# Convolution taps moved to ScalarE, and 14 pairs of up panels run with a seven-product block

## The chip, the cores and the metric

One core of one Trainium2 chip runs the whole program. The metric is the device time of one execution in microseconds (us), as the median of several runs. Engines: PE is TensorE, DVE is VectorE, ACT is ScalarE, POOL is GpSimd, SP is SyncE; a q behind a name (ACTq) marks the instruction queue of that engine issuing a transfer.

## The reference

Two decoder layers on 256 tokens of width 2048 in float32: a gated linear attention layer, then a forgetting attention layer, both with attention into 256 memory tokens. After each mixer comes the channel mixer, where the change lies:

```python
def causal_dwconv(u, w, b):
    s_ = u.shape[1]
    up = jnp.pad(u, ((0, 0), (CONV_WIDTH - 1, 0), (0, 0)))
    return w[0] * up[:, 0:s_] + w[1] * up[:, 1:s_ + 1] + w[2] * up[:, 2:s_ + 2] + b

def conv_ffn(h, w_up, conv_w, conv_b, w_down):
    u = causal_dwconv(h @ w_up, conv_w, conv_b)
    a, val = split_cols(u, [FFN_HIDDEN, FFN_HIDDEN])
    return (jax.nn.silu(a) * val) @ w_down
...
        h = rmsnorm(x, norm_ffn[i])
        x = x + conv_ffn(h, ffn_w_up[i], ffn_conv_w[i], ffn_conv_b[i], ffn_w_down[i])
```

The hidden width is 5632, so `w_up` has 11264 columns. Each channel of `u` gets three taps (weights w0, w1, w2 for the tokens two back, one back and the same) and a bias.

## The kernel before

**Units.** All weights stream from HBM as units: two blocks of 128 input features by 512 columns, one transfer of 512 KB into a tile `raw` (4 buffers). ACT rounds a unit to `whi` (L208, a cast to fp32r), DVE takes the rest, `wlo = raw - whi` (L217); `whi` and `wlo` have 3 buffers each. The tokens are held the same way, as a high and a low part. A block product of one 128x128 token block with a 128x512 weight block is then three matmuls (high by high, low by high, high by low), each 128x512. A plain unit has two feature blocks and two token blocks, so 4 block products, 12 matmuls.

**Panels.** A panel is 512 columns of a weight: 8 units for the 2048 input features, accumulated in two PSUM banks `acc` (one per token block; 4 banks in all, so two panels can be open). An up panel holds two blocks of 128 channels of the gate half and the two blocks of the value half that belong to them. There are 22 up panels in each layer; `PARTS` groups them 8, 8 and 6, and each part's down panels follow it.

**What happens to an up panel.** `panel(j, ...)` gives its evacuation: ACT scales both banks by the norm into `scaled` (2 buffers), DVE transposes 32x32 squares into `square`, ACT's queue writes that to DRAM (`turned`), and ACT's queue reads it back as channels by tokens into `u0` or `u1` (four transfers). Then `taken(j, base, u, i)`, once per half, does the convolution: per block one ACT instruction (tap 2 and bias, L1092) and two on DVE (taps 1 and 0, L1093 and L1094), Silu on ACT, the product on DVE, and the split into high and low parts as input of the down panels.

**What sets the order.** Each engine runs its queue strictly in order, and the transfers that ACT issues stand in the same queue as its arithmetic. The order of each queue is made by a list scheduler when the program is built; weight casts have a higher priority. `later((n, step), ...)` lets a step begin only behind the cast of the n-th unit from then: 3 for the write, 6 for the reads, 8 and 9 for the two halves of `taken`.

**Seven for eight.** `proj_seven` runs two panels at once, unit by unit, and uses all 4 `acc` banks. At chosen unit pairs (`forms`) it replaces the 8 block products of the pair by 7 on sums of blocks: 21 matmuls, not 24. Each panel's unit of the pair is loaded, four DVE instructions form the sums `t13` and `t24` (L346 to L349), and 3.5 tiles instead of 2 are cast and split (L314, L315: v0 whole, `vhi`/`vlo` half a tile, `t13`, `t24`). Four of the products go to PSUM banks of their own. `seven_evacuated` copies one of these to SBUF (`s16`), adds the others on DVE, and hands the sums to the evacuation, which adds them to the scaled panel (`extra`). Before the change this is used in the second layer's mixer and, with another ending (`add_seven`), in the down panels. All up panels run alone by `proj_tm` (two of each layer by `proj_two`).

Of the kernel before, what the change touches and what calls it, by code (L numbers as in the profile page):

```python
# [12 lines left out]
F32 = mybir.dt.float32  # L13
F32R = mybir.dt.float32r
I32 = mybir.dt.int32
AF = mybir.ActivationFunctionType
ALU = mybir.AluOpType
# [21 lines left out]
AHEAD = 300  # L39
SEVEN = ((3, 5), (3, 5, 7))  # L40
LAST = ()

SPREAD = [128 * q + 32 * k + i for k in range(4) for i in range(32) for q in range(4)]

# [93 lines left out]
def _trunk(ctx: ExitStack, tc: tile.TileContext, xt, xtok, memt, wp, wgu, gns, gfin, cnv, par, msk, out):  # L138
# [39 lines left out]
    def later(*steps):  # L178

        for units, step in steps:  # L180
            due.append([units, step])
# [267 lines left out]
    def back():  # L449
        return tp.tile([P, 4, T], F32, name="back", tag="back", bufs=2)  # L450
# [612 lines left out]
    def ffn(l, nx, h, m, then, ending=None):  # L1063
        with tc.tile_pool(name=f"ffn{l}", bufs=1) as fp, ExitStack() as ends:
# [11 lines left out]
            held = []  # L1076

            def spare_tile(name, dtype):
                return sp.tile([P, 512 if name in ("vhi", "vlo") else NUNIT], dtype, name=name, tag=name)

            def form(t):
                return lambda i: [t[:, h, i, :] for h in range(2)]

            def taken(j, base, u, i):

                cv = []
                for c in range(2):
                    v = u[:, 2 * c + i, :]
                    col = (c * 44 + j + i) * 4
                    w = [cw[:, col + n : col + n + 1] for n in range(4)]  # L1090
                    r = fp.tile([P, T], F32, name=f"cv{c}", tag=f"cv{c}", bufs=3)
                    S.activation(r, v[:, 2:], AF.Identity, bias=w[3], scale=w[2])  # L1092
                    V.scalar_tensor_tensor(r, v[:, 1 : T + 1], w[1], r, ALU.mult, ALU.add)  # L1093
                    V.scalar_tensor_tensor(r, v[:, :T], w[0], r, ALU.mult, ALU.add)  # L1094
                    cv.append(r)
                S.activation(cv[0], cv[0], AF.Silu)
                V.tensor_tensor(cv[1], cv[0], cv[1], ALU.mult)
                split(m, j + i - base, cv[1])
                if (j - base) // 2 in parts[base]:
                    held.append(cv[1])  # L1100
                    if i:
                        summed(parts[base][(j - base) // 2])

            def summed(form):
                ab = [natural(h)[:, :, b] for h in held for b in range(2)]
                held.clear()
                token_sums(*ab, sp.tile([P, 4, P], F32, name="sf", tag="sf"), [form[:, h, :, :] for h in range(2)])

            def panel(j, base, slack=0):
                held = []  # L1110

                def evac(b, a):
                    if not held:
                        held.append(Turn("turned"))
                    e = tp.tile([P, 512], F32, name="scaled", tag="scaled", bufs=2)
                    S.activation(e, a, AF.Copy, scale=nx.col()[:, b : b + 1])
                    held[0].put(b, e)
                    if not b:
                        return
                    u = us[turn[0] % 2]  # L1120
                    turn[0] += 1
                    later((3, held[0].write), (6, lambda: held[0].read(lambda k: u[:, k, 2:])),
                          (8 + slack, lambda: taken(j, base, u, 0)), (9 + slack, lambda: taken(j, base, u, 1)))

                return evac

            parts = {lo: dict(zip(SEVEN[1] if p < len(PARTS) - 1 else LAST, tiles)) for p, (lo, _) in enumerate(PARTS)}
            for p, (lo, hi) in enumerate(PARTS):
                forms = parts[lo]
                js = list(range(lo, hi, 2))  # L1130
                if not p:
                    proj_two([("up", l, j) for j in js[:2]], h, [panel(js[0], lo), panel(js[1], lo, 2)], 2)
                    js = js[2:]
                for j in js:
                    proj_tm(("up", l, j), h, panel(j, lo))
# [175 lines left out]
```

## Time and profile before

| | |
|---|---|
| time of the runs | median 2241.81 us (2240.89, 2241.81, 2243.47) |
| span of the profiled execution, first to last instruction | 2241.1 us; its time as a run is not listed apart |
| PE busy | 2227.2 us, 99% of the span |
| DVE busy | 1658.5 us, 74% |
| ACT busy | 1294.0 us, 58% |
| DMA | 516.98 MB, mean 231 GB/s |
| granted TensorE clock | 0.999 |

Busy time leaves out instructions that only wait or issue a transfer. Matmuls overlap in the pipeline, so the durations of single matmuls add up to more than the busy time.

### The profile page before, as it was taken

The numbers are of one execution on the slowest core, as the hardware profiler recorded it, in microseconds if no ns is written. First come the engines' busy times: TensorE is split into PE (matmuls) and PEld (weight loads), VectorE is DVE, ScalarE is ACT, GpSimd is POOL, SyncE is SP. The second block draws the span as 40 slices with busy tenths as digits, with TensorE's granted clock in tenths as the row PEclk, the third lists the DMA queues.
The fourth block names the chain that finished last, engine by engine and source line by source line (L and its number), as shares of the span: only waits on it lengthen the run. The fifth ranks groups of instructions, "written<-read, shape, count | busy, mean of one in ns | idle before, by whom it ended". The sixth has DMA issues, their size and how long they took to land.

```text
span 2241.1 us, 29637 instructions
## 1 busy us (share of the span) xinstructions
PE 2227.2 (99%) x10267; PEld 1860.8 (83%) x10267; DVE 1658.5 (74%) x2608; ACT 1294.0 (58%) x1921; POOL 44.6 (2%) x71
## 2 busy tenths in 40 slices
PE   9999999999999999999999999999999999999998
PEld 7888888888888888888888898888888888888886
DVE  7568887667689677886777875666778967787766
ACT  7555665656565465555656655555665555554654
POOL 0000000000000000000000000000000000000000
PEclk9999999999999999999999999999999999999999
DMA  9875667677875778667778777677876677767784
GB/s 319 277 234 188 205 208 224 202 234 242 256 222 201 243 233 249 213 203 246 235 254 263 243 239 222 196 233 244 255 243 220 204 239 244 240 193 233 237 242 150
DMA packets 276894, 516.98 MB, mean 231 GB/s; under 512 B 149884, under 2 KB 158600, under 8 KB 276616
## 3 DMA queue, kind: packets, MB, share of 16 engines
q1 hardware_dynamic: 124296, 427.24, 58.9%
q10 hardware_dynamic: 149760, 80.51, 12.6%
q0 software_dynamic: 2688, 7.34, 1.1%
q8 instruction: 80, 1.31, 0.2%
q14 instruction: 70, 0.57, 0.1%
HBM read 470.44 MB, written 44.58 MB: 230 GB/s over the span
## 4 chain that ended last, share of the span: by engine, by line
PE 95%; DMA 3%; DVE 1%; issue 1%; ACT 0%; SPq 0%; DVEq 0%; ACTq 0%
PE acc L229 24%; PE acc L230 24%; PE acc L233 24%; PE acc L291 16%; PE ps_s L291 1%; DMA back<-xturned 1%; PE ps_o L291 1%; PE ps_t L291 1%; DMA back<-turned 1%; DMA raw<-wp 1%; PE ps_s L833 0%; DMA turned<-square 0%; PE ps_s L634 0%; PE ps_t L623 0%; PE ps_o L645 0%
## 5 line engine op out<-in xcount | busy, mean ns | idle before, releaser
L217 DVE TENSOR_TENSOR wlo<-raw,whi 128x1024 fp32r<-128x1024 f32 (+4 forms) x763 | 912.6, 1199 | 458.0 <-ACT whi L208 429.5
L208 ACT ACTIVATE whi<-raw 128x1024 fp32r<-128x1024 f32 (+4 forms) x763 | 791.2, 1040 | 704.7 <-PE acc L230 471.9
L229 PE MATMUL acc<-whi,B 128*128 128x512 f32 (+3 forms) x1440 | 548.1, 382 | 0.0
L230 PE MATMUL acc<-whi,B 128*128 128x512 f32 (+3 forms) x1440 | 547.9, 382 | 0.0
L229 PE MATMUL acc<-whi,A 128*128 128x512 f32 x1120 | 437.3, 392 | 1.7 <-ACT whi L208 1.4
L230 PE MATMUL acc<-whi,A 128*128 128x512 f32 x1120 | 435.4, 390 | 0.0
L233 PE MATMUL acc<-wlo,B 128*128 128x512 f32 (+3 forms) x1440 | 377.0, 381 | 0.0
L229 PEld LDWEIGHTS acc<-whi,B 128*128 128x128 f32 x1440 | 270.3, 188 | 46.9
L230 PEld LDWEIGHTS acc<-whi,B 128*128 128x128 f32 x1440 | 269.9, 188 | 46.3
L233 PEld LDWEIGHTS acc<-wlo,B 128*128 128x128 f32 x1440 | 267.7, 188 | 46.4
L233 PE MATMUL acc<-wlo,A 128*128 128x512 f32 x1120 | 300.6, 390 | 0.3 <-DVE wlo L217 0.3
L229 PEld LDWEIGHTS acc<-whi,A 128*128 128x128 f32 x1120 | 210.3, 188 | 48.1 <-ACT whi L208 3.6
L233 PEld LDWEIGHTS acc<-wlo,A 128*128 128x128 f32 x1120 | 210.1, 188 | 44.3 <-DVE wlo L217 0.7
L230 PEld LDWEIGHTS acc<-whi,A 128*128 128x128 f32 x1120 | 210.3, 188 | 43.5 <-DVE A L527 0.2
L291 PE MATMUL acc<-whi,B 128*128 128x512 f32 x508 | 132.2, 390 | 0.0
L291 PE MATMUL acc<-whi,A 128*128 128x512 f32 x496 | 129.9, 390 | 0.0
L291 PEld LDWEIGHTS acc<-whi,B 128*128 128x128 f32 x508 | 95.1, 188 | 20.3
L1092 ACT ACTIVATE cv<-u,cw 128x256 f32<-128x256 f32 x176 | 96.8, 588 | 23.9 <-DMA u<-turned 23.9
L291 PEld LDWEIGHTS acc<-whi,A 128*128 128x128 f32 x496 | 93.1, 188 | 19.9
L314 ACT ACTIVATE whi<-t 128x1024 fp32r<-128x1024 f32 x46 | 48.9, 1062 | 79.2 <-DVE t L349 42.7
L1093 DVE SCALAR_TENSOR_TENSOR cv<-u,cw,cv 128x256 f32<-128x256 f32 x176 | 78.5, 479 | 15.6 <-ACT cv L1092 15.6
L438 DVE STREAM_TRANSPOSE square<-scaled 128x512 f32<-128x512 f32 x122 | 80.3, 692 | 0.0
(259 smaller groups left out, 1819.5 us busy)
## 6 DMA issues: line engine op xcount, KB each, us to landing
raw<-wp SPq DMA_DIRECT2D x743, 512.0 KB, 4.2
turned<-square ACTq DMA_DIRECT2D x61, 512.0 KB, 4.5
u<-turned ACTq DMA_DIRECT2D x176, 128.0 KB, 5.2
raw<-wp SPq DMA_DIRECT2D x32, 384.0 KB, 3.2
raw<-wp SPq DMA_DIRECT2D x24, 388.0 KB, 3.9
xturned<-square ACTq DMA_DIRECT2D x12, 512.0 KB, 4.3
back<-xturned ACTq DMA_DIRECT2D x40, 128.0 KB, 5.6
raw<-wp SPq DMA_DIRECT2D x8, 400.0 KB, 3.8
```

The lines of the kernel that those rows point to most:

```text
L208: casts.append(S.activation(hi[:, s], raw[:, s], AF.Copy))
L217: V.tensor_tensor(lo[:, s], raw[:, s], hi[:, s].bitcast(F32), ALU.subtract)
L229: TE.matmul(acc[:, :n], xh, hi[:, s], start=first and j == 0, stop=False)
L230: TE.matmul(acc[:, :n], xl, hi[:, s], start=False, stop=False)
L233: TE.matmul(a, xh, ls, start=False, stop=stop)
L291: TE.matmul(a[:, :n], x, w, start=k not in begun, stop=calls[k] == 0)
L314: casts.append(S.activation(hi, raw, AF.Copy))
L438: V.transpose(self.square[:, :, :, b], src.rearrange("p (c t) -> p c t", t=32))
L1092: S.activation(r, v[:, 2:], AF.Identity, bias=w[3], scale=w[2])
L1093: V.scalar_tensor_tensor(r, v[:, 1 : T + 1], w[1], r, ALU.mult, ALU.add)
```

## The change

Two things change in `ffn`, which both layers use.

The taps: a panel is now handled in whole tiles of 4 blocks. `begun` makes tap 2 with the bias into a tile `a` and tap 1 into a tile `b`, eight ACT instructions of 128x256, and one DVE addition of 128x1024; `taken` makes tap 0 into `b` (four more on ACT), adds it (DVE), and does Silu and product on half tiles of 128x512. `a` and `b` are the two buffers of `back`. The instructions with two constants are L1105, those with one L1107, the additions L1114 and L1119, Silu L1120, product L1121.

The pairs: after the first two up panels of a layer, up panels run two by two through `seven_evacuated`, the fifth unit pair (u = 4) with seven products, until two panels of the part are left, which run alone. That is 2, 3 and 2 pairs in the three parts of a layer, 14 in all. `mixed` holds the sums of token blocks that the seven products need, made once per layer. The two panels of a pair are written, read and tapped with two units more distance for the second (`slack`).

```diff
--- before.py
+++ after.py
@@ -39,6 +39,7 @@
 AHEAD = 300
 SEVEN = ((3, 5), (3, 5, 7))
 LAST = ()
+UP = (4,)
 
 SPREAD = [128 * q + 32 * k + i for k in range(4) for i in range(32) for q in range(4)]
 
@@ -1076,30 +1077,54 @@
             held = []
 
             def spare_tile(name, dtype):
-                return sp.tile([P, 512 if name in ("vhi", "vlo") else NUNIT], dtype, name=name, tag=name)
+                return sp.tile([P, NUNIT if name in ("t13", "t24") else 512], dtype, name=name, tag=name)
 
             def form(t):
-                return lambda i: [t[:, h, i, :] for h in range(2)]
-
-            def taken(j, base, u, i):
-
-                cv = []
+                return lambda i: [t[:, k, i, :] for k in range(2)]
+
+            mixed = [sp.tile([P, 2, 4, P], F32R, name=f"mixed{i}") for i in range(len(UP))]
+
+            def mixed_at(u, t):
+                def step():
+                    f, g = (tp.tile([P, 512], F32, name=n, tag="scaled", bufs=2) for n in ("sf", "sh"))
+                    sums_of(h, (2 * u, 2 * u + 1), f.rearrange("p (i t) -> p i t", t=P),
+                            g.rearrange("p (c t) -> p c t", t=T), [t[:, k, :, :] for k in range(2)])
+
+                return step
+
+            later(*[(18 + 2 * i, mixed_at(u, t)) for i, (u, t) in enumerate(zip(UP, mixed))])
+
+            def taps(t, u, j, n):
+
                 for c in range(2):
-                    v = u[:, 2 * c + i, :]
-                    col = (c * 44 + j + i) * 4
-                    w = [cw[:, col + n : col + n + 1] for n in range(4)]
-                    r = fp.tile([P, T], F32, name=f"cv{c}", tag=f"cv{c}", bufs=3)
-                    S.activation(r, v[:, 2:], AF.Identity, bias=w[3], scale=w[2])
-                    V.scalar_tensor_tensor(r, v[:, 1 : T + 1], w[1], r, ALU.mult, ALU.add)
-                    V.scalar_tensor_tensor(r, v[:, :T], w[0], r, ALU.mult, ALU.add)
-                    cv.append(r)
-                S.activation(cv[0], cv[0], AF.Silu)
-                V.tensor_tensor(cv[1], cv[0], cv[1], ALU.mult)
-                split(m, j + i - base, cv[1])
-                if (j - base) // 2 in parts[base]:
-                    held.append(cv[1])
-                    if i:
-                        summed(parts[base][(j - base) // 2])
+                    for i in range(2):
+                        k = 2 * c + i
+                        col = (c * 44 + j + i) * 4
+                        g = [cw[:, col + m : col + m + 1] for m in range(4)]
+                        if n == 2:
+                            S.activation(t[:, k, :], u[:, k, 2:], AF.Identity, bias=g[3], scale=g[2])
+                        else:
+                            S.activation(t[:, k, :], u[:, k, n : T + n], AF.Copy, scale=g[n])
+
+            def begun(j, u, got):
+                a, b = back(), back()
+                got += [a, b]
+                taps(a, u, j, 2)
+                taps(b, u, j, 1)
+                V.tensor_tensor(a, a, b, ALU.add)
+
+            def taken(j, base, u, got):
+                a, b = got
+                taps(b, u, j, 0)
+                V.tensor_tensor(a, a, b, ALU.add)
+                S.activation(a[:, :2, :], a[:, :2, :], AF.Silu)
+                V.tensor_tensor(a[:, 2:, :], a[:, :2, :], a[:, 2:, :], ALU.mult)
+                for i in range(2):
+                    split(m, j + i - base, a[:, 2 + i, :])
+                u = (j - base) // 2
+                if u in parts[base]:
+                    held.extend(a[:, 2 + i, :] for i in range(2))
+                    summed(parts[base][u])
 
             def summed(form):
                 ab = [natural(h)[:, :, b] for h in held for b in range(2)]
@@ -1109,18 +1134,20 @@
             def panel(j, base, slack=0):
                 held = []
 
-                def evac(b, a):
+                def evac(b, a, extra=None):
                     if not held:
                         held.append(Turn("turned"))
                     e = tp.tile([P, 512], F32, name="scaled", tag="scaled", bufs=2)
                     S.activation(e, a, AF.Copy, scale=nx.col()[:, b : b + 1])
+                    if extra is not None:
+                        V.scalar_tensor_tensor(e, extra, nx.col()[:, b : b + 1], e, ALU.mult, ALU.add)
                     held[0].put(b, e)
                     if not b:
                         return
-                    u = us[turn[0] % 2]
+                    u, got = us[turn[0] % 2], []
                     turn[0] += 1
                     later((3, held[0].write), (6, lambda: held[0].read(lambda k: u[:, k, 2:])),
-                          (8 + slack, lambda: taken(j, base, u, 0)), (9 + slack, lambda: taken(j, base, u, 1)))
+                          (8 + slack, lambda: begun(j, u, got)), (9 + slack, lambda: taken(j, base, u, got)))
 
                 return evac
 
@@ -1130,6 +1157,10 @@
                 js = list(range(lo, hi, 2))
                 if not p:
                     proj_two([("up", l, j) for j in js[:2]], h, [panel(js[0], lo), panel(js[1], lo, 2)], 2)
+                    js = js[2:]
+                while len(js) > 2:
+                    seven_evacuated([("up", l, j) for j in js[:2]], h, {u: form(t) for u, t in zip(UP, mixed)},
+                                    [panel(js[0], lo), panel(js[1], lo, 2)], spare_tile)
                     js = js[2:]
                 for j in js:
                     proj_tm(("up", l, j), h, panel(j, lo))
```

The instruction counts of the program: PE 9988 matmuls before, 9946 now; ACT 1788 and 2140; DVE 501 and 205 SCALAR_TENSOR_TENSOR, 1625 and 1823 TENSOR_TENSOR; transfers unchanged (SP 864, ACT 368).

How the queues change is shown at two places of the first layer's part 1: the handling of its first up panels, which before lies beside the next panels' plain units, and now beside the second pair of that part. Numbers behind names count buffers; `u0` and `u1` hold the panels, `cw` the taps' weights, `turned` is the DRAM copy.

First the queue of ACT. Before, from the write of a panel to the Silu of its first half:

```order
L441 DMA turned_6940<-square_6939 128x1024
L208 ACTIVATE whi_7023<-raw_7022 128x1024
L208 ACTIVATE whi_7041<-raw_7040 128x1024
L446 DMA u0_4583<-turned_6940 128x4x64 x4
L208 ACTIVATE whi_7063<-raw_7062 128x1024
L208 ACTIVATE whi_7081<-raw_7080 128x1024
L1092 ACTIVATE cv0_7086<-u0_4583,cw_4581 128x256
L1092 ACTIVATE cv1_7090<-u0_4583,cw_4581 128x256
L208 ACTIVATE whi_7121<-raw_7120 128x1024
L1092 ACTIVATE cv0_7126<-u0_4583,cw_4581 128x256
L1092 ACTIVATE cv1_7130<-u0_4583,cw_4581 128x256
L1096 ACTIVATE cv0_7086<-cv0_7086 128x256
```

Now, from the write of the first panel of the first pair to the last read of the second:

```order
L442 DMA turned_7140<-square_7139 128x1024
L209 ACTIVATE whi_7256<-raw_7255 128x1024
L447 DMA u0_4583<-turned_7140 128x4x64 x2
L442 DMA turned_7168<-square_7167 128x1024
L447 DMA u0_4583<-turned_7140 128x4x64 x2
L209 ACTIVATE whi_7278<-raw_7277 128x1024
L209 ACTIVATE whi_7300<-raw_7299 128x1024
L1105 ACTIVATE back_7305<-u0_4583,cw_4581 128x256 x2
L1107 ACTIVATE back_7306<-u0_4583,cw_4581 128x256 x2
L447 DMA u1_4584<-turned_7168 128x4x64 x3
L209 ACTIVATE whi_7329<-raw_7328 128x1024
L447 DMA u1_4584<-turned_7168 128x4x64
```

and on, through the fifth unit pair of the second pair:

```order
L1105 ACTIVATE back_7305<-u0_4583,cw_4581 128x256
L1107 ACTIVATE back_7306<-u0_4583,cw_4581 128x256
L1105 ACTIVATE back_7305<-u0_4583,cw_4581 128x256
L1107 ACTIVATE back_7306<-u0_4583,cw_4581 128x256
L315 ACTIVATE whi_7371<-raw_7361 128x1024
L315 ACTIVATE vhi_7375<-raw_7363 128x512
L1107 ACTIVATE back_7306<-u0_4583,cw_4581 128x256 x4
L315 ACTIVATE whi_7388<-t13_7365 128x1024
L1120 ACTIVATE back_7305<-back_7305 128x512
L381 ACTIVATE s16_7419<-ps_t_7357 128x512
L315 ACTIVATE whi_7398<-t24_7366 128x1024
```

Between the write and the first read stood two casts and stands one. Behind the reads stood the four taps of a panel with one cast between them; now twelve taps, the reads and the write of the other panel, Silu and `s16` stand among the casts of the fifth to the tenth unit (`whi_7256` to the cast of `t24`).

Then the queue of DVE at the same place. Before:

```order
L217 TENSOR_TENSOR wlo_7084<-raw_7080,whi_7081 128x1024
L1093 SCALAR_TENSOR_TENSOR cv0_7086<-u0_4583,cw_4581,cv0_7086 128x256
L1093 SCALAR_TENSOR_TENSOR cv1_7090<-u0_4583,cw_4581,cv1_7090 128x256
L1094 SCALAR_TENSOR_TENSOR cv0_7086<-u0_4583,cw_4581,cv0_7086 128x256
L1094 SCALAR_TENSOR_TENSOR cv1_7090<-u0_4583,cw_4581,cv1_7090 128x256
L217 TENSOR_TENSOR wlo_7124<-raw_7120,whi_7121 128x1024
L1093 SCALAR_TENSOR_TENSOR cv0_7126<-u0_4583,cw_4581,cv0_7126 128x256
L1093 SCALAR_TENSOR_TENSOR cv1_7130<-u0_4583,cw_4581,cv1_7130 128x256
L1097 TENSOR_TENSOR cv1_7090<-cv0_7086,cv1_7090 128x256
L1094 SCALAR_TENSOR_TENSOR cv0_7126<-u0_4583,cw_4581,cv0_7126 128x256
L1094 SCALAR_TENSOR_TENSOR cv1_7130<-u0_4583,cw_4581,cv1_7130 128x256
```

Now:

```order
L1114 TENSOR_TENSOR back_7305<-back_7305,back_7306 128x1024
L347 TENSOR_TENSOR t13_7365<-raw_7363,raw_7361 128x512
L348 TENSOR_TENSOR t13_7365<-raw_7363 128x512
L316 TENSOR_TENSOR wlo_7372<-raw_7361,whi_7371 128x1024
L316 TENSOR_TENSOR vlo_7376<-raw_7363,vhi_7375 128x512
L349 TENSOR_TENSOR t24_7366<-raw_7363,t13_7365 128x512
L1119 TENSOR_TENSOR back_7305<-back_7305,back_7306 128x1024
L316 TENSOR_TENSOR wlo_7389<-t13_7365,whi_7388 128x1024
L350 TENSOR_TENSOR t24_7366<-raw_7361,t24_7366 128x512
L1121 TENSOR_TENSOR back_7305<-back_7305 128x512
L316 TENSOR_TENSOR wlo_7399<-t24_7366,whi_7398 128x1024
```

The eight short tap instructions are gone; two additions of whole tiles stand ahead of `t13` and between the two steps of `t24`, on which the last cast of the fifth unit pair waits.

## The prediction

> **What bounds the kernel now.** I read the first part of the page, then the chain of work that ended last, then a window over the first layer's up and down panels.
>
> ```profile
> span 2241.1 us, 29637 instructions
> PE 2227.2 (99%) x10267; PEld 1860.8 (83%) x10267; DVE 1658.5 (74%) x2608; ACT 1294.0 (58%) x1921; POOL 44.6 (2%) x71
> ...
> PE 95%; DMA 3%; DVE 1%; issue 1%; ACT 0%; SPq 0%; DVEq 0%; ACTq 0%
> ```
>
> PE is never out of work and is 95% of the chain. The window from 512 to 1130 us (columns: window, length, then busy time and count of PE, weight loads, DVE, ACT, POOL; clock, DMA share, GB/s) gives the price of a matmul, and four plain up panels what DVE and ACT do beside it:
>
> ```profile
> 512.00:1130.00 618.00, 618.00 (x2722) 510.64 (x2721) 471.20 (x657) 357.44 (x471) 0.00 (x0) 1.00 0.74 232
> ...
> sum 85.33, PE 85.33 PEld 70.64 DVE 63.66 ACT 52.66 POOL 0.00; mean PE 21.33 PEld 17.66 DVE 15.92 ACT 13.17 POOL 0.00
> ```
>
> 618.00 us over 2722 matmuls is 0.227 us each, without a gap and at full clock. So a plain unit of 12 matmuls takes 2.72 us, and in this stretch only fewer matmuls can make the kernel faster, while every wait of PE makes it slower. The second row sums four panels (560.87 to 646.2 us): per panel DVE is busy 15.9 and ACT 13.2 of 21.3 us.
>
> **What the change removes.** 14 pairs times 3 matmuls are 42, as the program's count also says (9988 to 9946): 42 x 0.227 = **9.5 us** less on the path that sets the end. The profiled execution's span is 2241.1 us, 0.7 under the median of the runs; with every cost hidden the median would become 2232.3.
>
> **What it adds beside PE.** Prices come from places where instructions follow each other without idle time, start to start, since neighbours overlap by about 0.1 us. First ACT's timeline in a plain panel and in the second layer:
>
> ```profile
> 595.81 1.08 ACT L1092 ACTIVATE cv<-u,cw 128x256 f32<-128x256 f32 x2
> 596.80 0.40 ACT L1096 ACTIVATE cv<-cv 128x256 f32<-128x256 f32 x1
> 597.11 1.04 ACT L208 ACTIVATE whi<-raw 128x1024 fp32r<-128x1024 f32 x1
> ...
> 603.52 0.34 ACTq L441 DMA_DIRECT2D turned<-square  x1
> 604.51 1.06 ACT L208 ACTIVATE whi<-raw 128x1024 fp32r<-128x1024 f32 x1 [1.66 <-PE acc L230]
> 607.23 1.06 ACT L208 ACTIVATE whi<-raw 128x1024 fp32r<-128x1024 f32 x1 [1.66 <-PE acc L230]
> 608.41 2.14 ACTq L446 DMA_DIRECT2D u<-turned  x4
> ...
> 1234.20 1.05 ACT L208 ACTIVATE whi<-raw 128x1024 fp32r<-128x1024 f32 x1
> 1235.15 0.93 ACT L526 ACTIVATE A<-back,gains 128x256 fp32r<-128x256 f32 x2
> 1235.98 1.05 ACT L208 ACTIVATE whi<-raw 128x1024 fp32r<-128x1024 f32 x1
> ```
>
> A tap with two constants is 0.495 us (two in 0.99), one with one constant 0.415 (two of the like L526 in 0.83), a cast of a unit 0.95, a read 0.53 (four in 2.14). Half a cast I take as 0.53, the 0.63 of `vhi` below less the overlap. The read at 608.41 came 4.9 us behind its write at 603.52. Then DVE's, at a seven-product pair and at the end of a pair in the second layer:
>
> ```profile
> 1263.01 0.75 DVE L481 SCALAR_TENSOR_TENSOR scaled<-ps_t,ny,scaled 128x512 f32<-128x512 f32 x1
> 1263.67 0.74 DVE L481 SCALAR_TENSOR_TENSOR scaled<-s,ny,scaled 128x512 f32<-128x512 f32 x1
> 1264.34 0.71 DVE L438 STREAM_TRANSPOSE square<-scaled 128x512 f32<-128x512 f32 x1
> ...
> 1294.08 0.68 DVE L348 TENSOR_TENSOR t<-raw,t 128x512 f32<-128x512 f32 x1
> 1294.68 1.22 DVE L315 TENSOR_TENSOR wlo<-raw,whi 128x1024 fp32r<-128x1024 f32 x1
> 1295.82 0.68 DVE L349 TENSOR_TENSOR t<-raw,t 128x512 f32<-128x512 f32 x1
> 1296.42 2.52 DVE L315 TENSOR_TENSOR wlo<-t,whi 128x1024 fp32r<-128x1024 f32 x2
> ...
> L1093 DVE SCALAR_TENSOR_TENSOR cv<-u,cw,cv 128x256 f32<-128x256 f32 x176 | 78.5, 479 | 15.6 <-ACT cv L1092 15.6
> ```
>
> A whole tile of tensor by tensor is 1.14 us, half a tile 0.60, a scaled addition 0.67, an old tap 0.45 (78.5 us over 176).
>
> Per panel ACT gets 8 one-constant taps: +3.3 us; DVE loses 8 old taps (3.6) and gains two whole-tile additions (2.3): -1.3. Per pair the seven products cost ACT 1.5 casts and `s16` (0.95 + 0.53 + 0.5 = 2.0) and DVE four sums, 1.5 splits, four additions and four scaled additions (2.4 + 1.7 + 2.4 + 2.7 = 9.2). Reads and writes already cost ACT's queue about 2.5 us a panel. So in a pair's 189 x 0.227 = 42.9 us ACT has 2 x (13.2 + 2.5 + 3.3) + 2.0 = 40.0 us of work, before 31.4, and DVE 2 x (15.9 - 1.3) + 9.2 = 38.4, before 31.8. Both still fit; the average does not stop PE. The cover is thin, though, and both queues are strictly in order, so the place where things meet decides. SP's and POOL's queues keep their instructions. The sums `mixed`, 2 or 3 us of DVE once per layer, lie in the first plain panels and cost nothing beside 15.9 of 21.3.
>
> **The place: the fifth unit pair.** How the end of a pair passes shows where the second layer already has one (L479 is ACT's scaling of a finished panel, L441 the write, L446 a read), with PE's first matmul of the next pair:
>
> ```profile
> 1265.14 0.69 ACT L479 ACTIVATE scaled<-acc,ny 128x512 f32<-128x512 f32 x1 [0.63 <-DVE square L438]
> ...
> 1266.81 0.34 ACTq L441 DMA_DIRECT2D turned<-square  x1
> ...
> 1272.42 1.04 ACTq L446 DMA_DIRECT2D fkt<-turned  x2
> 1273.50 1.31 ACTq L441 DMA_DIRECT2D turned<-square  x1
> 1274.86 0.63 ACT L314 ACTIVATE vhi<-raw 128x512 fp32r<-128x512 f32 x1 [4.86 <-DVE t L346]
> ...
> 1264.16 1.07 PE L291 MATMUL acc<-whi,A 128*128 128x512 f32 x4
> ```
>
> Count from the next pair's first matmul, 1264.16. The write stands at +2.7, the reads at +8.3: ACT stood 4.86 us behind a read that waited for the write to land. It cost PE nothing there, since no taps followed. How long these transfers take over the kernel (last number, us to landing), and the writes in the window from 512 to 1130 us; and the idle time of PE (last number) ahead of the matmuls of pairs:
>
> ```profile
> turned<-square ACTq DMA_DIRECT2D x61, 512.0 KB, 4.5
> u<-turned ACTq DMA_DIRECT2D x176, 128.0 KB, 5.2
> ...
> DMA to landing us min/median/max: 2.4/4.9/9.9
> ...
> L291 PE MATMUL acc<-whi,B 128*128 128x512 f32 x508 | 132.2, 390 | 0.0
> ```
>
> Now I walk the new order of part 1's second pair with these prices, in us from that pair's first matmul. Before the write stand the evacuation of the second panel and a cast that needs the first unit's buffer (free at +2.3): write at +3.4. Landed, by 4.9, at +8.3. First two reads, second panel's write, two more reads: to +10.7. Casts of units 6 and 7: to +12.6. First tap at 8.3 + 5.2 = +13.5; four taps 1.8: +15.3. Three reads of the second panel, the first under the last tap: +16.6. Cast of unit 8: +17.55. Four taps: **+19.4**. Only now can DVE begin its row: addition 1.14, the two steps of `t13` 1.2, split 1.14, half split 0.6, first step of `t24` 0.6, second addition 1.14, split of `t13` 1.14, second step of `t24` 0.6, in all 7.56: +27.0. The cast of `t24`, 0.95 and a tenth to be seen: **+28.0**. PE wants it behind 8 units and 14 matmuls, 110 x 0.227 = +24.95. PE so waits **3.1 us**, and the time is not regained, for in the rest of the pair PE has no slack. DVE's own 7.56 us leave nothing to hide: had the taps ended by +16.3, PE would not wait.
>
> The same sequence (addition, `t13`, `t24` around the second addition) stands in DVE's queue at four pairs of each layer, those that follow another pair: 8 x 3.1 = **24.8 us**. Their two kinds differ a little: at the third pair of part 1 the write stands behind one cast more, about 0.5 us later, with no cast between it and the reads. The first pair of a layer follows `proj_two`, whose first panel is finished 5.4 us earlier; its addition stands well ahead, and a late Silu between the steps of `t24` may cost 0 to 1.5, I take 0.8: 1.6 for both. The first pairs of the other two parts, four in all, meet no taps: 0.
>
> **The plain panels behind a pair.** The taps of a pair's second panel fall into the first plain panel, 6 such places. There casts have their usual cushion (3 buffers, about 5 us) and no sum to wait for, but ACT carries 13.2 + 2.5 + 3.3 = 19.0 of 21.8 us and two panels' reads. The trace shows no such load. From below the cost is 0, as in every plain panel now; from above it is one landing less the cushion that is left, 2 us. I take 1: **6 us**. Where the taps meet down panels, the walk leaves casts just in time: 0, up to 1 each.
>
> **The sum.** -9.5 + 24.8 + 1.6 + 6 = +22.9; 2241.8 + 22.9 = **2265 us**, 1.0% slower.
>
> **Rivals.** (1) *The gain arrives*, 2232.3 us. It takes one thing: the round trip through DRAM (4.9 + 5.2 us in my walk) shorter by 3.1 us, so that the taps end by +16.3. For it: a landing as short as 2.4 us occurs, and PE has not waited at a pair until now (0.0 in the L291 row). Against: the medians 4.5 and 5.2, the 4.9 at 603.52 and 5.6 at 1266.81. From the point where the wait is 1.2 us a pair, 9.5 us in all with nothing else, the gain wins. The Trainium skill, "DMA: Bandwidth & Descriptors", section "Anatomy of one DMA", gives a transfer as 2.0 us plus its bytes by 436 GB/s (a fit for the GpSimd path): by that page an estimate of 3.2 us for the write and 2.3 for a read, 4.6 less than my round trip, and the kernel would be faster. The rows above disagree with it for these small-piece transfers in a busy stretch, so I give this rival little. (2) *Even*: a wait of about 1.2 us a pair, 2242. Halfway values of the landing do that. (3) *Worse*: ACT at 19.0 of 21.8 us also fails in the plain panels and down panels (14 places more at 2 to 3 us): 2265 + 35 = 2300. For it: each late read stops casts behind it. Against: 5 us of cushion. That the change takes out fewer matmuls than said is excluded by the count.
>
> **How the numbers follow.** The forecast, waits of 2 to 5 us at the eight pairs, 0.58: from -9.5 + 16 + 0 + 2 = +8.5 to -9.5 + 40 + 3 + 10 = +43, so 2250 to 2285. The gain 0.15, even 0.12, worse 0.15. Faster by over 0.2% (about what this kernel's measurement can tell from no change, 4.5 us) 0.15, within it 0.12, slower 0.73. The range reaches down to the whole gain, 2233, and up to 2292 in the worse case.
>
> **What the next profile would show.** If right: PE's pitch still 0.227, its count 42 lower; idle time of PE ahead of matmuls with `whi` or `ps_o` at the cast line of `t24` (now L315), released by ACT, about 3 us each at eight places; ACT's queue standing behind `u<-turned` some 5 us behind each write; DVE in one run of 7 to 8 us from the first whole-tile addition to the second step of `t24`. If the reads follow their writes by 3 us or less, or the first addition ends before +17 of a pair, I am wrong at the landing; if DVE idles between the addition and `t24`, at the order.

## The result and the profile after

The changed kernel takes **2274.7 us** (median; 2271.1 to 2279.8), the kernel before 2242.6 (2240.9 to 2244.3) in the same comparison: a ratio of **1.014**, 95% interval 1.0126 to 1.0155. It is slower, by 32 us of the medians and 28.2 of the profiled spans, where 23 were forecast. The page of the profiled execution, its first part and the chain of work that ended last:

```profile
span 2269.3 us, 29661 instructions
...
PE 2232.2 (98%) x10225; PEld 1853.6 (82%) x10225; DVE 1749.1 (77%) x2510; ACT 1446.1 (64%) x2273; POOL 44.6 (2%) x71
...
PE 82%; DMA 5%; DVE 5%; ACT 5%; issue 2%; ACTq 1%; SPq 0%; DVEq 0%
```

The 42 matmuls are gone (10267 before; both traces count 279 more than the program's own list of matmuls). PE's share of the chain fell from 95% to 82%: stretches of the chain now run through DVE, ACT and transfers, though PE is still busy 98% of the span. That is the look of many short waits.

To size them I add up, from the trace, the start-to-start distances of successive matmuls beyond a full-speed pitch of 0.2268 us. This excess is 24.8 us before and 62.3 after: +37.5, less 42 x 0.227 = 9.5, is +28.0, which is the spans' 28.2. I split it into the **eight** fifth unit pairs of the pairs that follow a pair (from 4 us ahead of the first product with `mixed` to 3 us behind the last) and the **rest**. After, the eight hold 24.9 us and the rest 37.4, 12.6 more than before.

One of the eight, part 1's second pair, whose first matmul is at 773.03 us. A selection of its timeline (start, duration, engine, line; in brackets the idle time ahead and what ended it), with rows of ACT, DVE and PE in order of time:

```profile
775.63 0.34 ACTq L442 DMA_DIRECT2D turned<-square  x1
781.49 0.93 ACTq L447 DMA_DIRECT2D u<-turned  x2
785.31 2.01 ACT L209 ACTIVATE whi<-raw 128x1024 fp32r<-128x1024 f32 x2 [6.43 <-DMA raw<-wp]
787.48 1.13 ACT L1105 ACTIVATE back<-u,cw 128x256 f32<-128x256 f32 x2 [0.16 <-DMA u<-turned]
...
793.39 0.49 ACT L1107 ACTIVATE back<-u,cw 128x256 f32<-128x256 f32 x1
793.91 1.23 DVE L1114 TENSOR_TENSOR back<-back 128x1024 f32<-128x1024 f32 x1 [0.56 <-ACT back L1107]
795.06 0.69 DVE L347 TENSOR_TENSOR t<-raw 128x512 f32<-128x512 f32 x1
796.26 1.22 DVE L316 TENSOR_TENSOR wlo<-raw,whi 128x1024 fp32r<-128x1024 f32 x1
797.53 0.50 PE L292 MATMUL ps_t<-wlo,B 128*128 128x512 f32 x1 [0.98 <-DVE wlo L316]
798.60 1.22 DVE L1119 TENSOR_TENSOR back<-back 128x1024 f32<-128x1024 f32 x1
799.73 1.22 DVE L316 TENSOR_TENSOR wlo<-t,whi 128x1024 fp32r<-128x1024 f32 x1
800.87 0.69 DVE L350 TENSOR_TENSOR t<-raw,t 128x512 f32<-128x512 f32 x1
801.01 0.73 PE L292 MATMUL ps_s<-wlo,mixed 128*128 128x512 f32 x2 [1.57 <-DVE wlo L316]
801.59 1.06 ACT L315 ACTIVATE whi<-t 128x1024 fp32r<-128x1024 f32 x1 [0.62 <-DVE t L350]
802.70 0.58 PE L292 MATMUL ps_o<-whi,mixed 128*128 128x512 f32 x1 [0.95 <-ACT whi L315]
803.50 0.63 PE L292 MATMUL ps_o<-whi,mixed 128*128 128x512 f32 x1
```

From the pair's first matmul: write +2.6, first read +8.5, first tap +14.5, first addition +20.9, then one unbroken run on DVE to the second step of `t24`, whose cast starts 7.7 us behind the first addition and ends at +29.6. PE starts on it at +29.7 and has by then waited three times, for the splits of the unit, of `t13`, and for this cast.

### The profile page after: what moved, and what is told of

It reads as the page before. It is cut to its first block, busy times and chain, and to the rows that moved or that the text cites. A ratio compares the mean times of both kernels' runs of the same rounds, so it can differ in the third digit from the quotient of the medians.

```text
span 2269.3 us, 29661 instructions
## 1 busy us (share of the span) xinstructions
PE 2232.2 (98%) x10225; PEld 1853.6 (82%) x10225; DVE 1749.1 (77%) x2510; ACT 1446.1 (64%) x2273; POOL 44.6 (2%) x71
## 4 chain that ended last, share of the span: by engine, by line
PE 82%; DMA 5%; DVE 5%; ACT 5%; issue 2%; ACTq 1%; SPq 0%; DVEq 0%
PE acc L292 32%; PE acc L230 15%; PE acc L231 15%; PE acc L234 15%; DMA turned<-square 2%; PE ps_s L292 1%; ACT whi L209 1%; PE ps_o L292 1%; ACT back L1105 1%; ACT back L1107 1%; DVE wlo L316 1%; DMA raw<-wp 1%; DMA back<-xturned 1%; ACTq L447 1%; DVE wlo L218 1%
## 5 line engine op out<-in xcount | busy, mean ns | idle before, releaser
L218 DVE TENSOR_TENSOR wlo<-raw,whi 128x1024 fp32r<-128x1024 f32 (+4 forms) x735 | 873.9, 1196 | 327.6 <-ACT whi L209 287.5
L230 PE MATMUL acc<-whi,B 128*128 128x512 f32 (+3 forms) x992 | 373.8, 379 | 0.2 <-ACT scaled L1141 0.2
L231 PE MATMUL acc<-whi,B 128*128 128x512 f32 (+3 forms) x992 | 373.5, 379 | 0.0
L292 PE MATMUL acc<-whi,B 128*128 128x512 f32 x1320 | 339.0, 392 | 3.6 <-ACT whi L209 3.6
L292 PE MATMUL acc<-whi,A 128*128 128x512 f32 x1308 | 336.5, 391 | 2.7 <-ACT whi L209 2.7
L230 PE MATMUL acc<-whi,A 128*128 128x512 f32 x672 | 263.0, 395 | 2.0 <-ACT whi L209 1.7
L231 PE MATMUL acc<-whi,A 128*128 128x512 f32 x672 | 261.4, 392 | 0.0
L234 PE MATMUL acc<-wlo,B 128*128 128x512 f32 (+3 forms) x992 | 257.9, 378 | 0.0
L234 PEld LDWEIGHTS acc<-wlo,B 128*128 128x128 f32 x992 | 183.7, 188 | 28.9
L234 PE MATMUL acc<-wlo,A 128*128 128x512 f32 x672 | 181.6, 390 | 0.2 <-DVE wlo L218 0.2
L292 PE MATMUL acc<-wlo,B 128*128 128x512 f32 x660 | 181.7, 390 | 0.0
L292 PE MATMUL acc<-wlo,A 128*128 128x512 f32 x654 | 180.8, 390 | 0.0
L1107 ACT ACTIVATE back<-u,cw 128x256 f32<-128x256 f32 x352 | 153.3, 495 | 5.4 <-DVE back L1114 4.0
L234 PEld LDWEIGHTS acc<-wlo,A 128*128 128x128 f32 x672 | 126.1, 188 | 26.8 <-DVE wlo L218 0.7
L292 PEld LDWEIGHTS acc<-wlo,B 128*128 128x128 f32 x660 | 124.1, 188 | 25.9
```

The costliest lines, as they stand in the source:

```text
L218: V.tensor_tensor(lo[:, s], raw[:, s], hi[:, s].bitcast(F32), ALU.subtract)
L230: TE.matmul(acc[:, :n], xh, hi[:, s], start=first and j == 0, stop=False)
L231: TE.matmul(acc[:, :n], xl, hi[:, s], start=False, stop=False)
L234: TE.matmul(a, xh, ls, start=False, stop=stop)
L292: TE.matmul(a[:, :n], x, w, start=k not in begun, stop=calls[k] == 0)
L1107: S.activation(t[:, k, :], u[:, k, n : T + n], AF.Copy, scale=g[n])
```

## The experiments

All ratios are to the kernel before, run on the same chip (its own row is from the first comparison). Beside the experiments the kernel before took 2244.1 to 2244.4, so medians of different rows compare to about 2 us. "Eight" and "rest" are the excess in us, as above, each from one profiled execution, which lies up to 5.7 us from its kernel's median.

| kernel | us, median (range) | ratio (95%) | eight | rest |
|---|---|---|---|---|
| before | 2242.6 (2240.9 to 2244.3) | 1 | – | 24.8 |
| after | 2274.7 (2271.1 to 2279.8) | 1.0140 (1.0126 to 1.0155) | 24.9 | 37.4 |
| taps alone | 2251.5 (2248.3 to 2255.4) | 1.0034 (1.0022 to 1.0046) | – | 33.9 |
| pairs alone | 2281.1 (2278.2 to 2284.7) | 1.0164 (1.0148 to 1.0179) | 33.1 | 38.1 |
| taps later | 2296.2 (2292.0 to 2300.2) | 1.0230 (1.0214 to 1.0246) | 8.0 | 78.4 |
| reads by POOL | 2240.4 (2237.4 to 2246.8) | 0.9984 (0.9972 to 0.9997) | 2.7 | 29.3 |
| only the queue | 2281.8 (2277.6 to 2286.3) | 1.0166 (1.0144 to 1.0188) | 34.4 | 40.3 |
| only the order | 2249.4 (2245.9 to 2255.1) | 1.0026 (1.0015 to 1.0036) | 10.9 | 28.4 |
| before, reads by POOL | 2246.3 (2243.0 to 2250.9) | 1.0009 (0.9999 to 1.0018) | – | 28.9 |
| taps alone, reads by POOL | 2279.4 (2269.1 to 2284.8) | 1.0152 (1.0120 to 1.0184) | – | 65.1 |
| second addition later | 2266.8 (2260.6 to 2269.5) | 1.0097 (1.0078 to 1.0116) | 21.4 | 35.9 |
| sums first | 2254.5 (2249.0 to 2260.2) | 1.0047 (1.0029 to 1.0065) | 9.0 | 42.3 |
| sums first, reads by POOL | **2239.8** (2235.6 to 2243.2) | 0.9978 (0.9968 to 0.9989) | 0.8 | 26.0 |
| taps that wait for no transfer | 2259.3 (2254.5 to 2263.0) | 1.0065 (1.0043 to 1.0086) | 21.0 | 30.5 |

**Each half alone.** First the taps without pairs:

```diff
-            later(*[(18 + 2 * i, mixed_at(u, t)) for i, (u, t) in enumerate(zip(UP, mixed))])
...
-                while len(js) > 2:
+                while len(js) > 99:
```

> All up panels run alone again, only the taps are the new ones; 9988 matmuls as before. Theory (PE waits because the taps' whole-tile addition stands in DVE's queue ahead of the sums of the fifth unit pair, late by the DRAM round trip): no sums, so nothing waits: 2240 to 2248 us, and no PE gap over 1 us at an up panel. Rival (ACT simply has too much work, 19 of 21.8 us per panel): plain panels stall too, 2255 us or more.

It is 0.34% slower, between the two expectations: 9 us more of excess, half of it in down panels and 4.1 us at one place of the second layer's first up panels (a wait of 2.3 us and slow matmuls behind it). Then the pairs with the old taps on DVE (with two buffers for the gate half's tile, where before had three):

```diff
-                          (8 + slack, lambda: begun(j, u, got)), (9 + slack, lambda: taken(j, base, u, got)))
+                          (8 + slack, lambda: taken(j, base, u, 0)), (9 + slack, lambda: taken(j, base, u, 1)))
```

> The 14 pairs with the old taps (one ACT and two DVE instructions per block; cv0 with 2 buffers instead of 3 for space). Theory: DVE then carries 8 short taps per panel in the same place (3.6 us instead of 2.3), but half of them behind the sums of t24; the waits at the eight pairs stay, at 1 to 4 us each: 2245 to 2270. Rival (the taps on ACT are the cause): the gain arrives, 2232 to 2238.

The rival falls: the waits stand at the same eight places, 33.1 us, and the time is above even the theory's range. So the new taps do not make the waits (with them the eight hold 8 us less, though the buffers differ too); the pairs do, with the handling of a panel laid across the fifth unit pair.

**Where in the pair.** The paired panels' taps moved 4 units later:

```diff
-                                    [panel(js[0], lo), panel(js[1], lo, 2)], spare_tile)
+                                    [panel(js[0], lo, 4), panel(js[1], lo, 6)], spare_tile)
```

> The change with the taps of paired panels four units later (12 and 13, 14 and 15 behind the evacuation instead of 8 and 9, 10 and 11), behind the fifth unit pair. The same work on every engine. Theory: the eight waits go (23 us of the changed kernel's PE gaps with the slow matmuls behind them); what is left are down panels and the rest: 2243 to 2254. Rival (load): 2268 to 2280, the waits only move.

Slower than either said. The eight shrink to 8.0 us, as theory had it, but the rest grows by 41. Two places of it, in the timeline:

```profile
688.49 1.98 PE L292 MATMUL acc<-whi,A 128*128 128x512 f32 x4 [3.81 <-ACT A L524]
...
852.25 2.06 ACT L1105 ACTIVATE back<-u,cw 128x256 f32<-128x256 f32 x4
854.21 1.69 ACT L1107 ACTIVATE back<-u,cw 128x256 f32<-128x256 f32 x4
856.91 1.45 PE L292 MATMUL acc<-whi,B 128*128 128x512 f32 x5 [1.04 <-ACT whi L209]
```

Eight taps in one line, 3.7 us, now hold a cast of the next plain units, and a part's down panels wait 3.8 us for their last input (`A`), which the later taps make later.

**The reads off ACT's queue.** My theory by then was ACT's queue: it stands 5 us and more behind a write that has not landed, with casts behind it.

```diff
-                    later((3, held[0].write), (6, lambda: held[0].read(lambda k: u[:, k, 2:])),
+                    later((3, held[0].write), (6, lambda: held[0].read(lambda k: u[:, k, 2:], queue=nc.gpsimd)),
```

> The change with the reads of u issued by POOL instead of ACT; ACT no longer stands behind the landing of the write, and has 2.1 us of issue less per panel. Theory: casts and taps start at the landing, some 2 to 4 us earlier in a pair, the waits at the eight pairs halve or go: 2240 to 2262. Rival (DVE's order alone sets the wait, wherever the taps lie): 2268 to 2278.

34 us faster than the changed kernel; the theory seemed shown. But the scheduler had also rebuilt the order of every queue: at the eight places DVE now makes `t24` ahead of the second addition. Two kernels take these apart. In both the orders of PE, DVE, ACT and SP are held by edges between each instruction and the next, taken from another kernel's program:

```diff
+        for a, b in zip(queue, queue[1:]):
+            tc.add_manual_dep(b, a.name, info, reason="held")
```

Only the queue: reads by POOL, the order of the changed kernel.

> The changed kernel with one thing moved: POOL issues the 176 reads of u. The order of every other instruction on PE, DVE, ACT and SP is held as it stands in the changed kernel (the sums t13 and t24 still stand behind and around the two whole-tile additions). Theory, ACT's queue standing behind the write's landing is the cause: the taps then end about 3 us earlier in a pair (no 2.1 us of reads in ACT's queue, no standing of casts behind them), the waits at the fifth unit pair fall from about 2.5 us to under 1 us each, 2238 to 2252. Rival, the order on DVE is the cause: with that order kept the waits stay, 2262 to 2276.

Only the order: reads on ACT, the order of the kernel with POOL's reads.

> The other half: the reads of u stay in ACT's queue, but PE, DVE, ACT and SP keep for all other instructions the order that the kernel with POOL's reads has, in which t24 is made ahead of the second addition at the pairs that follow a pair (a gain of 1.14 us of DVE at each by the walk, 2.28 where the first addition too stands behind t24's first step). Theory, ACT's queue is the cause: the casts of t13 and t24 stand behind the reads all the same, 2258 to 2272. Rival, the order on DVE is the cause: 2238 to 2250.

The theory of ACT's queue **falls** as the main cause: without the order the queue gives nothing (7 us slower, with intervals that overlap), and the order alone brings 25 of the 34 us. The other 9 come from the queue, once the order is there. Why the free queue did not help, at part 1's third pair of the queue-only kernel:

```profile
830.75 2.97 POOL L447 DMA_DIRECT2D u<-turned  x4 [41.84 <-DMA turned<-square]
...
836.20 0.60 ACT L1105 ACTIVATE back<-u,cw 128x256 f32<-128x256 f32 x1 [4.72 <-DMA u<-turned]
837.55 0.60 ACT L1105 ACTIVATE back<-u,cw 128x256 f32<-128x256 f32 x1 [0.74 <-DMA u<-turned]
...
850.50 0.76 PE L292 MATMUL ps_o<-whi,mixed 128*128 128x512 f32 x1 [0.96 <-ACT whi L315]
```

POOL takes 0.74 us to issue a read, ACT 0.53; ACT now stands behind the data in place of the issue. At the second pair, where the taps did end 2.6 us earlier (+18.3, not +20.9), the excess fell from 6.2 to 2.1 us; at the third it rose from 2.2 to 6.8.

**Reads by POOL elsewhere.** The same edit in the kernel before, and in the taps without pairs:

> The kernel before, with POOL issuing the 176 reads of u, nothing else. Theory: PE never waited for them there, so 2239 to 2246, no change. Rival, taking reads off ACT's queue is worth time by itself whatever the taps and pairs do: 2225 to 2236.

> The new taps without any pairs (2251.5 us with the reads in ACT's queue, most of its new idle time of PE in the down panels), with POOL issuing the reads. Theory, these waits too come from ACT's queue standing behind the write: they go, 2241 to 2246. Rival, they come from ACT's load of taps itself or from the two buffers of whole tiles: 2249 to 2254.

Nothing in the one, as theory had it. In the other both expectations were low: 28 us slower than with ACT's reads. The order of the queues was free here, so how much of this is the reads' and how much the order's is not shown. One place of its timeline:

```profile
838.09 0.60 ACT L1105 ACTIVATE back<-u,cw 128x256 f32<-128x256 f32 x1 [0.58 <-DMA u<-turned]
...
839.06 0.60 ACT L1105 ACTIVATE back<-u,cw 128x256 f32<-128x256 f32 x1 [0.37 <-DMA u<-turned]
...
841.66 1.99 ACT L209 ACTIVATE whi<-raw 128x1024 fp32r<-128x1024 f32 x2
...
842.75 0.50 PE L230 MATMUL acc<-whi,B 128*128 128x512 f32 x1 [1.04 <-ACT whi L209]
```

The taps stand one by one behind reads that arrive one by one, and casts behind the taps. The kernel with POOL's reads is 28 us slower here, and 9 faster where the order is held and suits them (2249.4 to 2240.4 above).

**The row on DVE.** The new theory: PE waits for the row of DVE from the first addition to the last step of `t24`. In the first test everything is held in the changed kernel's order, but the second addition moves (with Silu and product, which would stop the cast and split of `t24`):

```diff
 L349 TENSOR_TENSOR t_7366<-raw,t_7365 128x512
-L1119 TENSOR_TENSOR back<-back 128x1024
 L316 TENSOR_TENSOR wlo<-t_7365,whi 128x1024
 L350 TENSOR_TENSOR t_7366<-raw,t_7366 128x512
-L1121 TENSOR_TENSOR back<-back 128x512
+L1119 TENSOR_TENSOR back<-back 128x1024
 L316 TENSOR_TENSOR wlo<-t_7366,whi 128x1024
+L1121 TENSOR_TENSOR back<-back 128x512
```

> The changed kernel's order held on every queue, but for one step at the eight pairs that follow a pair: the second whole-tile addition moves from between the two steps of t24 to behind the second (with Silu on ACT and the product on DVE behind the cast and split of t24, which they would otherwise stop). The reads stay in ACT's queue. Theory, the row on DVE from the first addition to t24 sets the wait: the cast of t24 comes 1.1 us earlier at each of the eight, 9 us in all, 2262 to 2268. Rival, it is ACT's queue and the landings, the row on DVE only fills the wait: 2271 to 2278.

In the theory's range: 7.9 us less by the medians, 5.0 by the spans. At the eight themselves the excess fell by 3.5 us (24.9 to 21.4), where 9 were expected: at part 2's second pairs the taps ended a microsecond later (+20.1 and +20.2, not +19.1 and +19.0). At part 1's second pair the row from the first addition to the cast's start is 6.55 us, not 7.68; half a microsecond is given back a unit later (a wait of 0.46 us for the next cast, behind Silu now). Then, in the program, both additions of a pair's first panel behind `t24`:

```diff
-                V.tensor_tensor(t24[:, n:], r0[:, n:], t24[:, :n], ALU.subtract)
+                t24s[:] = [V.tensor_tensor(t24[:, n:], r0[:, n:], t24[:, :n], ALU.subtract)]
...
+            def added(got):
+                a, b = got
+                with tc.issue_after(t24s[-1].ins):
+                    V.tensor_tensor(a, a, b, ALU.add)
...
+                        later((8, lambda: begun(j, u, got, False)), (10, lambda: added(got)),
+                              (11, lambda: taken(j, base, u, got)))
```

> Written in the program, order free elsewhere: at the pairs that follow a pair both whole-tile additions of the first panel are issued behind the second step of t24 (tap 0 then 2 units later). The reads stay in ACT's queue. Theory, the row on DVE: the casts of t13 and t24 no longer stand behind any addition; t24's cast waits only for the casts and splits ahead of it, and about 1 us is left at each of eight pairs: 2238 to 2250. Rival, ACT's queue and the landings: 2262 to 2276. A third possibility, that tap 0 moved 2 units later stops casts at the end of the pair as the later taps did: 2252 to 2262, with the idle time behind the pairs.

> The same with POOL issuing the reads of u. Theory: with the row on DVE gone, the reads' place matters little in the pairs; it can take the last microsecond (the eight waits of about 1 us) or, where POOL's slower issue makes taps late, cost as much: 2232 to 2244. Rival, each issue by POOL costs more than it gives, as in the kernel without pairs: 2250 or more.

With ACT's reads the eight fall from 24.9 to 9.0 us, and the time to 2254.5. That is above the theory's range and in that of the third possibility, but no wait of over 0.35 us stands in the rest of those pairs, where it was expected: most of what is left is elsewhere (42.3 us, some of it in stages that the edit does not touch). With POOL's reads, the order again free, the eight are gone, the rest is near that of the kernel before (26.0 and 24.8), and the median is the lowest of all: 0.22% under before, with an interval that overlaps that of POOL's reads alone. Its page, and the second pair in its timeline (first matmul at 768.35; the additions are L1120 and L1125 here):

```profile
span 2233.8 us, 29816 instructions
...
PE 2220.9 (99%) x10225; PEld 1853.1 (83%) x10225; DVE 1746.2 (78%) x2510; ACT 1448.6 (65%) x2273; POOL 175.0 (8%) x247
...
PE 95%; DMA 2%; DVE 2%; ACT 1%; issue 1%; ACTq 0%; SPq 0%; DVEq 0%
```

```profile
785.76 0.69 DVE L347 TENSOR_TENSOR t<-raw 128x512 f32<-128x512 f32 x1 [2.20 <-DMA raw<-wp]
...
788.71 0.68 DVE L350 TENSOR_TENSOR t<-raw,t 128x512 f32<-128x512 f32 x1
789.31 1.22 DVE L1120 TENSOR_TENSOR back<-back 128x1024 f32<-128x1024 f32 x1
789.50 1.06 ACT L315 ACTIVATE whi<-t 128x1024 fp32r<-128x1024 f32 x1 [1.27 <-DVE t L350]
...
793.09 0.39 PE L292 MATMUL ps_o<-whi,mixed 128*128 128x512 f32 x1
```

`t13` starts at +17.4, when its unit has landed, and not behind an addition; the cast of `t24` ends at +22.2, and PE takes it up at +24.7 without a wait (by the walk PE comes to it at +24.95).

**The landing.** Last, the other end of the walk. The taps read a constant tile and need no transfer:

```diff
-                            S.activation(t[:, k, :], u[:, k, 2:], AF.Identity, bias=g[3], scale=g[2])
+                            S.activation(t[:, k, :], mask[:, 2 : T + 2], AF.Identity, bias=g[3], scale=g[2])
...
-                            S.activation(t[:, k, :], u[:, k, n : T + n], AF.Copy, scale=g[n])
+                            S.activation(t[:, k, :], mask[:, n : T + n], AF.Copy, scale=g[n])
```

> The changed kernel, but the taps read a constant tile of the same form and not u, so that they need no transfer to have landed (the output is then not the reference's; every transfer and every instruction is still there, and the reads still stand in ACT's queue). Order free. At the pairs that follow a pair the DVE queue still has the first addition ahead of t13 and the second ahead of the last step of t24. Theory, the taps' end (two landings behind the write) and the row on DVE together set the wait: the taps now end about 3 us earlier, so most of the wait of the eight pairs goes even with the row in place, 2236 to 2254. Rival, the row on DVE and ACT's load of taps do it by themselves, whenever the data is there: 2260 to 2276.

15 us faster than the changed kernel, just under the rival's range. Of the eight, 21.0 of 24.9 us stay; most of the gain is in the rest. The order was free, and it moved. Part 1's second pair (first matmul at 770.69):

```profile
787.73 1.23 DVE L1114 TENSOR_TENSOR back<-back 128x1024 f32<-128x1024 f32 x1 [2.15 <-ACT back L1107]
788.42 1.06 ACT L209 ACTIVATE whi<-raw 128x1024 fp32r<-128x1024 f32 x1 [0.73 <-PE acc L292]
...
789.52 1.23 DVE L218 TENSOR_TENSOR wlo<-raw,whi 128x1024 fp32r<-128x1024 f32 x1 [0.56 <-ACT whi L209]
790.66 0.69 DVE L347 TENSOR_TENSOR t<-raw 128x512 f32<-128x512 f32 x1
...
793.60 1.22 DVE L1119 TENSOR_TENSOR back<-back 128x1024 f32<-128x1024 f32 x1
796.47 0.68 DVE L350 TENSOR_TENSOR t<-raw,t 128x512 f32<-128x512 f32 x1
...
798.36 0.50 PE L292 MATMUL ps_o<-whi,mixed 128*128 128x512 f32 x1 [1.02 <-ACT whi L315]
```

The eight taps now end at +17.0 and the first addition is over at +18.3. Still `t13` starts only at +20.0 (+22.0 in the changed kernel): ahead of it in DVE's queue, now behind the first addition, stands the split of the eighth unit, whose cast waits for PE to free a buffer. From there the row has 5.8 us to the last step of `t24`, the second addition in it, as before, and PE waits again.

The second layer's part 0 shows the same where the taps are earlier still (its second pair's first matmul is at 1614.41):

```profile
1630.32 1.23 DVE L1114 TENSOR_TENSOR back<-back 128x1024 f32<-128x1024 f32 x1 [2.16 <-ACT back L1107]
1631.46 1.22 DVE L218 TENSOR_TENSOR wlo<-raw,whi 128x1024 fp32r<-128x1024 f32 x1
1633.02 0.69 DVE L347 TENSOR_TENSOR t<-raw 128x512 f32<-128x512 f32 x1 [0.34 <-DMA raw<-wp]
...
1640.73 0.50 PE L292 MATMUL ps_o<-whi,mixed 128*128 128x512 f32 x1 [0.79 <-ACT whi L315]
```

The taps end at +15.9, but the split of the eighth unit and then the landing of the weights hold `t13` to +18.6, and PE still waits.

## Why the prediction was right, point by point

- **Fewer matmuls, 9.5 us: right.** 10267 to 10225, and in the best kernel, whose excess is 2.0 us above that of before, the span is 7.3 us under before (4.4 by the medians).
- **The eight pairs, 24.8 us: right in place, and in sum (24.9) closer than the walk deserved.** The second pairs of the parts hold 1.6, 6.2 and 2.9 us in the first layer, 1.4, 5.4 and 2.9 in the second, the third pair of part 1 2.2 and 2.3; forecast were 3.1 each. The pair that was walked holds 6.2, twice its forecast, and smaller ones make up for it: that the sums agree to 0.1 us is luck. The two large ones include 1.4 us each of matmuls at nearly twice their pitch (0.43 us).
- **The walk: right to about 1.5 us.** Forecast and measured: write +3.4 and +2.6, reads +8.3 and +8.5, first tap +13.5 and +14.5, eight taps done +19.4 and +20.9, DVE's row to the cast 7.56 and 7.7, the cast's end +28.0 and +29.6. The reads stand 5.9 us behind the write, not 4.9. One thing I did not see: PE waits at the splits of the unit and of `t13` first, since both stand in the same row.
- **"Had the taps ended by +16.3, PE would not wait": wrong.** This step failed, although the forecast held. With no landing to wait for, the taps end at +15.6 and +15.9 at two of the eight pairs, and PE waits there all the same (0.8 and 1.2 us of excess); at the other six they end at +17.0 to +18.4. By the walk that leaves some 7 us of waits at the eight; 21.0 us of excess stayed. The walk took DVE's row to begin with the taps' end. It left out the split of the eighth unit, which at six of the eight stands between the first addition and `t13`, and in the changed kernel at two (part 0's second pairs: taps done at +16.7 and +16.5, excess 1.6 and 1.4 us). So rival 1 (a shorter round trip brings the gain) had too simple a condition; since the order was free in that run, how much of the wait an earlier landing would take away in the changed kernel's own order stays open. The estimates of 3.2 and 2.3 us that the Trainium skill, "DMA: Bandwidth & Descriptors", section "Anatomy of one DMA", led to, were far from this trace, which has the medians below. What the runs show to matter is the row: 1.14 us less of it in each pair gave 7.9 us of the median, with the order held but for that addition and what hangs on it, and the additions out of it, with POOL's reads, took all but 0.8 us of the eight.

```profile
turned<-square ACTq DMA_DIRECT2D x61, 512.0 KB, 4.6
u<-turned ACTq DMA_DIRECT2D x176, 128.0 KB, 5.1
```

- **The first pair of a layer, 1.6 us: 0.2 at the place named** (0.1 in each layer), and 1.3 in the units behind it (541.8 and 1607.4 us).
- **The plain panels behind a pair, 6 us: too much.** Two waits, 0.8 us in all. **The down panels, 0: too little.** Five waits of 0.9 to 1.7 us, 6.1 in all, one of them:

```profile
933.51 1.66 PE L292 MATMUL acc<-whi,A 128*128 128x512 f32 x6 [1.56 <-ACT whi L209]
```

  The two errors cancel, by luck. The taps alone show where the cost falls: what I put on the plain panels is felt in the down panels, half of its 9 us without any pair. That it is the load of taps on ACT, and not the two buffers or the whole-tile additions, is not shown. The rest of the shortfall, some 4 us of 28 by the spans, lies in small waits of other stages (1296.4 and 1536.5 us are the largest), and I did not settle it.

So the forecast came out in direction, place and range because its largest term was taken from the right row of DVE. It was 9 us low by the medians and 5 by the spans, its terms agree better in sum than one by one, and its account of what would lift the largest term failed.

## What to carry to other kernels

Where an engine's queue is strictly in order, ask of each step that the tensor engine waits for what stands ahead of it although it could come later: here two additions of 1.14 us stood ahead of sums whose inputs had landed some 3 us before, and those sums make the next weights. Moving a transfer to an idle engine also moves the scheduler's order; hold the order before you credit the queue. An average that fits (40 of 42.9 us) says little where two strict queues meet at one place.

## What the runs showed of the hardware

Short waits can cost clock. Windows of the changed kernel (length, PE, weight loads, DVE, ACT, POOL busy; clock, DMA share, GB/s):

```profile
512.00:1145.00 633.00, 621.47 (x2709) 507.70 (x2708) 518.93 (x616) 430.66 (x642) 0.00 (x0) 1.00 0.72 226
794.00:806.00 12.00, 8.49 (x29) 5.84 (x28) 10.52 (x12) 9.42 (x16) 0.00 (x0) 0.87 0.48 150
```

Behind the three waits at 797.5 to 802.7 us seven matmuls follow at a pitch of 0.43 us (803.50 and on), with the granted clock at 0.87 in that window, although no single wait was over 1.8 us. The Trainium skill, "TensorE: Matmul & The Clock Gate", section "Why this matters for your kernels", warns of idle gaps over about 3 us; here waits that add up to 4.0 us, in pieces within some 6 us, did the same. In the kernel with the taps alone one wait of 2.26 us (up to 1608.38) was enough: six matmuls at 0.43 us follow, with a granted clock of 0.76 from 1606 to 1613. Two waits of 2.6 us together at 1065.8 to 1067.5 us of the changed kernel were followed by none, so no length seen here decides by itself.

A read of 128 KB in small pieces lands no sooner from POOL. The queues of the changed kernel (packets, MB, share of the DMA engines), then of the kernel with POOL's reads:

```profile
q10 hardware_dynamic: 149760, 80.51, 12.4%
q0 software_dynamic: 2688, 7.34, 1.1%
```

```profile
q10 hardware_dynamic: 56832, 57.43, 7.9%
q0 software_dynamic: 11136, 30.42, 5.1%
...
u<-turned POOLq DMA_DIRECT2D x176, 128.0 KB, 5.1
```

The same 176 reads are 92928 packets on ACT's queue and 8448 on POOL's, 528 and 48 each; the median landing is 5.1 us in both.
